# All HGRN2 heads through the levels together: scores by half chunks, mask copies over all partitions

## Chip, cores and metric

The kernel runs on one core of a Trainium2 chip. The metric is the device time of one execution in microseconds; the reported time is the median of three runs. In the trace the engines are PE (TensorE's matmuls), PEld (its weight loads), DVE (VectorE), ACT (ScalarE), POOL (GpSimd) and SP (SyncE, which issues most of the DMAs).

## What is computed

The reference is a trunk of two layers on 512 tokens of width 1024, all in float32. Each layer adds the output projection of three token mixers (RG-LRU, retention and HGRN2) to x, and then a gated feed-forward block with a short convolution.

```python
for l in range(DEPTH):
    proj = rmsnorm(x, norm1_w[l]) @ w_in[l]
    lx, lg, rq, rk, rv, rg, hq, hf, hi, hg = jnp.split(proj, split_idx, axis=-1)
    y_lru = rglru_group(lx, lg, ...)
    y_ret = retention_group(rq, rk, rv, rg, ret_norm_w[l])
    y_hg = hgrn2_group(hq, hf, hi, hg, lb_all[l], hg_norm_w[l])
    x = x + jnp.concatenate([y_lru, y_ret, y_hg], axis=-1) @ w_out[l]
    x = x + conv_ffn(rmsnorm(x, norm2_w[l]), ...)
return rmsnorm(x, final_norm_w)
```

HGRN2 has four heads of width 64. With a forget gate f, keys k, queries q and values v its recurrence is S_t = diag(f_t) S_{t-1} + k_t v_t^T, and the output is o_t = S_t^T q_t. Retention has the same form with a fixed decay for each head. Both outputs are normalised for each head and gated.

## The kernel before

**Precision and projections.** A large product is made of three fp32r matmuls (`mm3`, lines 319 to 321): high times high, high times low and low times high. `split_w` splits every weight tile into a high part (ACT, `wh`) and a low part (DVE, `wl`). An input projection takes 24 matmuls of 512 columns per tile of 128 outputs; there are 24 tiles in a layer, in the order of `WIN` (line 63). Four PSUM banks (`NMM`) hold projections until `evac` multiplies them by the norm of the tokens and writes them to one of four `ev` tiles. All other matmuls are plain float32 and go through `small` (line 325). Each such product stands in the trace as two instructions.

**Order.** `Flow` is a planner: Python generators (chains) yield between operations, and every operation has an assumed cost (`Timed`). The main chain issues the large matmuls; whenever a chain's operands are due by the planner's clock, its small matmuls are put into TensorE's order between two of the large ones. Each engine executes its list in that order. If an operand is later on the chip than was planned, TensorE waits with everything behind it.

**HGRN2.** `hg_chain(ft)` runs once for each of two pairs of heads; a pair fills the 128 partitions (64 per head). Scores inside a chunk of 128 tokens are built in seven levels (`LEVELS` 1, 2, ... 64). At each level 8 products (4 at level 64) of the keys with every second block of queries go to the PSUM tile `hg_pl`. GpSimd then multiplies half of the keys by products of forget gates (`kl`), VectorE multiplies half of the queries (`qr`) and the gates by each other (`p2`), and VectorE writes the scores under a mask into `st` by `copy_predicated`, once for each half of the partitions. The next level's products need the new keys and queries. Behind the levels come `key_rows` (transposes, `k_tps`), `states` (`k_mps`, `k_sv`), `mix_values` (`k_o`) and a norm over each head (`head_norm`).

**The rest of a mixer stage.** Retention (`ret_chain`, for each pair of heads) needs rotated queries and keys (`rope`), forms scores per head (`rt_ps`), and shares `states` and `mix_values`; its norm (`head_norm_cols`) computes a reciprocal root on a few columns (`hc_rc`, `rsqrt_cols`) and spreads it by products with the identity (`hn_rps`). The LRU (`lru_conv`, `lru_batch`, `scan`) starts its convolutions when both HGRN2 pairs are done; at its end GpSimd multiplies four tiles (`qp<-qp,lr_g` in the trace, line 850) ahead of four VectorE scans.

**Ends.** The last layer's last down projection (`down_and_norm`) runs in two halves of the tokens; `finish` computes the reciprocal root of the final norm on two columns (`fn_v`, `fn_rc`), spreads it (`fn_rps`), scales x and stores it. At the start `FIRST` (line 31) is the order of the first loads: tiles of x and halves of the first two weight tiles.

## Time and profile before

| | us |
|---|---|
| median of three runs | 1194.06 |
| lowest and highest run | 1193.67, 1194.18 |
| profiled execution, its own time | 1192.48 |
| its span, first to last instruction | 1190.7 |
| PE busy in the span | 1171.8 |
| DVE busy | 810.9 |
| ACT busy | 511.3 |
| POOL busy | 101.9 |

Busy times are unions of an engine's instructions. Matmuls are pipelined: one that follows another starts before its predecessor has ended, and the distance from start to start is what it costs. The two layers have the same stages: mixers with the input projection (from 6.32 and 594.80 us), the output projection (from 191.75 and 773.48 us), and the feed-forward block.

### The profile page before, as it was taken

To read this page: it belongs to the slowest core of one execution; us is meant where nothing else is said; L and a number is where in the kernel's file an instruction comes from. 1 tells how busy PE (TensorE), PEld (TensorE's weight loads), DVE (VectorE), ACT (ScalarE), POOL (GpSimd) and SP (SyncE) were. 2 spreads that over 40 slices of the span, in tenths; PEclk is the share of its full clock that TensorE was granted. 3 is DMA by queue.
4 is the path that set the end of the run, shared out by engine and by line. 5 is a ranking of instruction groups with operands and counts; after the bars stand their busy time and mean duration, and the time that the engine had idled before them with its cause. 6 is when DMAs were issued, how large, how long until landed. Compare 5 with 4: busy or idle time off the path is not lost.

```text
span 1190.7 us, 15377 instructions
## 1 busy us (share of the span) xinstructions
PE 1171.8 (98%) x6062; PEld 968.4 (81%) x6062; DVE 810.9 (68%) x1220; ACT 511.3 (43%) x689; POOL 101.9 (9%) x85
## 2 busy tenths in 40 slices
PE   9999989999999999999999999999999999999996
PEld 8787778888888888888897877788888888888886
DVE  7998678667775576465679775964877646655746
ACT  6425574454443343242441446644544423433423
POOL 0221230000000000000323111400000000000001
PEclk9999999999999999999999999999999999999998
DMA  7222213233323322322332121323232233233221
GB/s 257 92 81 64 80 42 118 89 97 98 103 79 96 112 92 81 117 83 80 115 124 63 63 89 54 98 97 107 89 104 91 80 115 96 81 107 102 80 83 73
DMA packets 36312, 112.29 MB, mean 94 GB/s; under 512 B 4496, under 2 KB 4752, under 8 KB 36240
## 3 DMA queue, kind: packets, MB, share of 16 engines
q1 hardware_dynamic: 34416, 108.95, 29.2%
q10 hardware_dynamic: 1824, 2.37, 0.7%
q8 instruction: 47, 0.77, 0.3%
q14 instruction: 25, 0.20, 0.1%
HBM read 107.10 MB, written 2.10 MB: 92 GB/s over the span
## 4 chain that ended last, share of the span: by engine, by line
PE 92%; DVE 5%; issue 1%; DMA 0%; POOL 0%; ACT 0%; POOLq 0%; ACTq 0%
PE pps L319 19%; PE pps L321 18%; PE pps L320 18%; PE dps L319 7%; PE dps L321 7%; PE dps L320 7%; PE ops L321 2%; PE ops L320 2%; PE ops L319 2%; DVE qp L185 2%; PE k_o L325 1%; PE vps L319 1%; PE lr_ps L325 1%; DVE st L185 1%; PE vps L320 1%; PE vps L321 1%
## 5 line engine op out<-in xcount | busy, mean ns | idle before, releaser
L319 PE MATMUL pps<-xh,wh 128*128 128x512 f32 x1024 | 406.3, 397 | 1.3 <-ACT wh L185 1.3
L321 PE MATMUL pps<-xh,wl 128*128 128x512 f32 x1024 | 399.3, 390 | 0.6 <-DVE wl L185 0.6
L320 PE MATMUL pps<-xl,wh 128*128 128x512 f32 x1024 | 399.1, 390 | 0.0
L185 ACT ACTIVATE wh<-raw 128x1024 fp32r<-128x1024 f32 (+3 forms) x211 | 204.7, 973 | 145.8 <-PE dps L320 103.3
L185 DVE TENSOR_TENSOR wl<-raw,wh 128x1024 fp32r<-128x1024 f32 (+3 forms) x211 | 242.6, 1153 | 20.4 <-ACT wh L185 19.8
L319 PEld LDWEIGHTS pps<-xh,wh 128*128 128x128 f32 x1024 | 192.5, 188 | 44.4 <-issue 2.9
L321 PEld LDWEIGHTS pps<-xh,wl 128*128 128x128 f32 x1024 | 192.4, 188 | 42.0 <-DVE wl L185 1.2
L320 PEld LDWEIGHTS pps<-xl,wh 128*128 128x128 f32 x1024 | 192.5, 188 | 39.7 <-issue 1.2
L185 DVE SCALAR_TENSOR_TENSOR hs<-pps,rb 128x512 f32<-128x512 f32 x88 | 60.5, 691 | 128.7 <-PE pps L321 128.7
L319 PE MATMUL dps<-gh,wh 128*128 128x512 f32 x320 | 124.5, 389 | 0.0
L320 PE MATMUL dps<-gl,wh 128*128 128x512 f32 x320 | 124.5, 389 | 0.0
L321 PE MATMUL dps<-gh,wl 128*128 128x512 f32 x320 | 124.5, 389 | 0.0
L185 DVE TENSOR_TENSOR x<-x,dps 128x512 f32<-128x512 f32 (+1 forms) x72 | 45.1, 627 | 107.3 <-PE dps L321 106.6
L185 ACT ACTIVATE cg<-hs,prm 128x512 f32<-128x512 f32 x44 | 35.9, 817 | 81.1 <-DVE hs L185 76.4
L320 PEld LDWEIGHTS dps<-gl,wh 128*128 128x128 f32 x320 | 60.1, 188 | 12.5
L321 PEld LDWEIGHTS dps<-gh,wl 128*128 128x128 f32 x320 | 60.1, 188 | 12.5
L319 PEld LDWEIGHTS dps<-gh,wh 128*128 128x128 f32 x320 | 60.1, 188 | 12.4
L185 DVE SCALAR_TENSOR_TENSOR cvv<-hs,prm,cvv 128x511 f32<-128x511 f32 x88 | 65.9, 748 | 1.8
L185 DVE SCALAR_TENSOR_TENSOR cg<-hs,prm,cg 128x511 f32<-128x511 f32 x88 | 65.8, 748 | 1.5
L185 ACT ACTIVATE cg<-cg 128x512 f32<-128x512 f32 x44 | 27.8, 632 | 86.9 <-DVE cg L185 86.9
L185 ACT ACTIVATE gh<-cvv 128x512 fp32r<-128x512 f32 x44 | 27.8, 631 | 76.6 <-DVE cvv L185 76.6
L185 ACT ACTIVATE cvv<-hs,prm 128x512 f32<-128x512 f32 x44 | 35.9, 817 | 33.0 <-DVE hs L185 33.0
(210 smaller groups left out, 1353.3 us busy)
## 6 DMA issues: line engine op xcount, KB each, us to landing
raw<-in_wup_dram SPq DMA_DIRECT2D x88, 512.0 KB, 3.5
raw<-in_win_dram SPq DMA_DIRECT2D x46, 512.0 KB, 3.5
raw<-in_wdn_dram SPq DMA_DIRECT2D x48, 384.0 KB, 3.0
raw<-in_wout_dram SPq DMA_DIRECT2D x16, 512.0 KB, 3.5
raw<-in_wdn_dram SPq DMA_DIRECT2D x16, 256.0 KB, 2.6
x<-in_x_dram SPq DMA_DIRECT2D x8, 256.0 KB, 5.0
sw<-ev ACTq DMA_DIRECT2D x32, 64.0 KB, 2.5
out_dram<-hs SPq DMA_DIRECT2D x7, 256.0 KB, 2.0
```

The source lines that it names most:

```text
L185: return fn(*args, **kw)
L319: T.matmul(out=ps, lhsT=ah, rhs=bh, start=start, stop=False)
L320: T.matmul(out=ps, lhsT=ah, rhs=bl, start=False, stop=False)
L321: T.matmul(out=ps, lhsT=al, rhs=bh, start=False, stop=stop)
L325: T.matmul(**kw)
```

## The change

HGRN2 is rebuilt for all four heads at once. The projections of both pairs' gates and queries (`hf`, `hq`) stand ahead of the HGRN2 values in `WIN`. `hg_query(ft)` prepares the queries of a pair; one `hg_chain` runs the levels over tiles `qa`, `fa`, `ka`, `sta` that hold both pairs side by side. A level has 16 products in one PSUM bank (8 at level 64, which alternate between the two halves of the partitions). Scores stand in `sta` by half chunks: both halves of a chunk use the same 64 columns on their own 64 partitions, so that one `copy_predicated` covers all 128 partitions; level 32 is copied by ACT without a mask. The product with the values is therefore also made by half chunks, against values `vz` with zeros in the other half. The key products `kl` and the product of queries and keys move from POOL to DVE, as do the four products ahead of the LRU's scans.

Retention's scores are issued with the two heads of a pair in turn, into two PSUM banks. Its states are products of full width whose cross terms are multiplied by zero, so the product with the state is also one of full width. `head_norm_cols` writes the last step of the reciprocal root spread over 64 columns (`hx`) and uses products of full width.

`finish` takes a square root on ACT and a reciprocal and one correction step on DVE; the table of the square root is loaded at the first tile of the last down projection. The output tiles have buffers of their own, the scaling on ACT is done as x becomes known, and the last store is split in two, on two queues. The first weight half is loaded from SP's queue. A smaller scratch area of the DMAs frees memory for the pool `low`, which holds `hx`, `r_sv` and `vz`. The planner's price of `copy_predicated` is raised.

```diff
 WIN = (
-    [("f", 2304), ("f", 2048), ("v", 2560, 0), ("v", 2560, 1), ("f", 2432), ("f", 2176)]
+    [("f", 2304), ("f", 2048), ("f", 2432), ("f", 2176), ("v", 2560, 0), ("v", 2560, 1)]
     + [("f", 1024), ("f", 1280), ("v", 1536, 0), ("v", 1536, 1), ("f", 1152), ("f", 1408)]
...
 WNAMES = (
-    [("hf", 0), ("hq", 0), "hv", None, ("hf", 1), ("hq", 1)]
+    [("hf", 0), ("hq", 0), ("hf", 1), ("hq", 1), "hv", None]
     + [("rq", 0), ("rk", 0), "rv", None, ("rq", 1), ("rk", 1)]
...
-    hc = rsqrt_cols(mp, ps, [128, NC, 2], "hc", bufs=2)
+    hx = low.tile([128, NC, 2, 64], F32, name="hc_x")
+    rsqrt_cols(mp, ps, [128, NC, 2], "hc", bufs=2, out=hx)
...
     for c in range(NC):
-        for h in range(2):
-            small(0.12, out=ps[64 * h:64 * h + 64, c * 128:(c + 1) * 128],
-                  lhsT=hc[:, c, h:h + 1].to_broadcast([128, 64]), rhs=ident, skip_group_check=True)
+        small(0.22, out=ps[:, c * 128:(c + 1) * 128],
+              lhsT=hx[:, c].rearrange("p h n -> p (h n)"), rhs=ident)
...
+    for c in range(1, NC):
+        cs = slice(c * 128, (c + 1) * 128)
+        small(0.22, out=ops[:, cs], lhsT=sv[:, c - 1, :], rhs=q[:, cs],
+              start=c == 1, stop=False, skip_group_check=True)
...
-            hs = slice(64 * h, 64 * h + 64)
-            small(0.11, out=ops[hs, cs], lhsT=sv[hs, c - 1, :], rhs=q(c, h),
...
+qa = mp.tile([128, 2, 2 * S], F32, name="qp")
+fa = mp.tile([128, 2 * S], F32, name="f")
+ka = mp.tile([128, 2 * S], F32, name="k")
+
+
+sta = mp.tile([128, 4 * NC, 128], F32, name="st")
...
-    qk = mp.tile([128, S], F32, name="sq", bufs=2)
-    G.tensor_tensor(out=qk, in0=q, in1=kt, op=ALU.mult)
+    yield None
+    qk = sg
+    V.tensor_tensor(out=qk, in0=q, in1=ka[:, ts], op=ALU.mult)
+    V.tensor_tensor(out=q, in0=q, in1=fa[:, ts], op=ALU.mult)
+    yield None
     for h in range(2):
         hs = slice(64 * h, 64 * h + 64)
-        V.tensor_tensor(out=qp[hs, h, :], in0=q[hs, :], in1=f[hs, :], op=ALU.mult)
+        A.activation(out=qa[hs, h, ts], in_=q[hs, :], func=AF.Copy)
...
+def hg_chain():
+    for ft in range(2):
+        yield has(("hq", ft))
+    p = fa
...
+            pl = yield from psum([128, NB, 2, 32], "hg_pl")
+        for c in range(NB):
+            for b in range(1 if s == 64 else 2):
+                m = 64 * (c % 2) if s == 64 else 64 * b
+                q0 = c * 128 + 64 * b
+                n = 128 if s == 64 else 64
+                rhs = qa[:, :, q0:q0 + n].rearrange("p h (b t s) -> p h b t s", t=2, s=s)[:, :, :, 1, :]
+                small(0.1 if s == 64 else 0.05,
+                      out=pl[m:m + 64, c // 2 if s == 64 else c].rearrange("p h (b s) -> p h b s", s=s),
+                      lhsT=ka[:, q0:q0 + 64], rhs=rhs, skip_group_check=True)
...
+        nb2 = S // s
         pv = p[:, 0:2 * nb2].rearrange("p (b t) -> p b t", t=2)
-        kl = kt.rearrange("p (b t s) -> p b t s", t=2, s=s)[:, :, 0, :]
-        G.tensor_tensor(out=kl, in0=kl, in1=pv[:, :, 1:2].to_broadcast([128, nb2, s]), op=ALU.mult)
-        go = fl.mark
-        fl.mark, fl.last = fl.now, None
-        qr = qp.rearrange("p h (b t s) -> p h b t s", t=2, s=s)[:, :, :, 1, :]
+        kl = ka.rearrange("p (b t s) -> p b t s", t=2, s=s)[:, :, 0, :]
+        V.tensor_tensor(out=kl, in0=kl, in1=pv[:, :, 1:2].to_broadcast([128, nb2, s]), op=ALU.mult)
+        qr = qa.rearrange("p h (b t s) -> p h b t s", t=2, s=s)[:, :, :, 1, :]
         V.tensor_tensor(out=qr, in0=qr,
                         in1=pv[:, :, 0].unsqueeze(1).unsqueeze(3).to_broadcast([128, 2, nb2, s]), op=ALU.mult)
-        go = max(go, fl.mark)
-        p2 = mp.tile([128, S // 2], F32, name=f"hg_p{ft}", bufs=2)
+        go = fl.mark
+        p2 = mp.tile([128, S], F32, name="hg_p", bufs=2)
         V.tensor_tensor(out=p2[:, 0:nb2], in0=pv[:, :, 0], in1=pv[:, :, 1], op=ALU.mult)
         if s == 64:
-            A.activation(out=st[0:64, :, 64:128], in_=pl[0:64].rearrange("p c h t -> p (c h) t"), func=AF.Copy)
+            for m in range(2):
+                A.activation(out=sta[0:64].rearrange("p (c m h) q -> p c m h q", m=2, h=2)[:, :, m, :, 64:128],
+                             in_=pl[64 * m:64 * m + 64], func=AF.Copy)
+        elif s == 32:
+            for m in (0, 64):
+                A.activation(out=sta[m:m + 32, :, 32:64], in_=pl[m:m + 32].rearrange("p c h q -> p (c h) q"),
+                             func=AF.Copy)
         else:
-            for m in (0, 64):
-                V.copy_predicated(
-                    out=st[m:m + 64, :, m:m + 64].rearrange("p g (b t s) -> p g b t s", t=2, s=s)[:, :, :, 1, :],
-                    mask=msk[m:m + 64, i, :].rearrange("p (b s) -> p b s", s=s).unsqueeze(1).to_broadcast(
-                        [64, NC * 2, 32 // s, s]),
-                    data=pl[m:m + 64].rearrange("p c h (b s) -> p (c h) b s", s=s),
-                )
+            V.copy_predicated(
+                out=sta[:, :, 0:64].rearrange("p g (b t s) -> p g b t s", t=2, s=s)[:, :, :, 1, :],
+                mask=msk[:, i, :].rearrange("p (b s) -> p b s", s=s).unsqueeze(1).to_broadcast(
+                    [128, 2 * NB, 32 // s, s]),
+                data=pl.rearrange("p c h (b s) -> p (c h) b s", s=s),
+            )
         drop(sm)
         p = p2
         if s == 1:
-            evt.add(("f_free", ft))
+            evt.add("f_free")
         yield go - fl.now
...
+    pss = []
+    for ft in range(2):
+        pss.append((yield from psum([128, S], "k_o")))
+    for ft in range(2):
+        ops = pss[ft]
+
+        for b in range(2):
+            for c in range(NC):
+                for h in range(2):
+                    d0 = (2 * ft + h) * 64
+                    small(0.1, out=ops[64 * h:64 * h + 64, c * 128 + 64 * b:(c + 1) * 128],
+                          lhsT=vz[:, c, b, d0:d0 + 64], rhs=sta[:, ft * NB + 2 * c + h, 0:128 - 64 * b],
+                          start=b == c == 0, stop=False, skip_group_check=True)
+        for c in range(1, NC):
+            for h in range(2):
+                small(0.11, out=ops[64 * h:64 * h + 64, c * 128:(c + 1) * 128], lhsT=sv[:, ft, c - 1, :],
+                      rhs=qa[:, h, ft * S + c * 128:ft * S + (c + 1) * 128],
+                      start=False, stop=False, skip_group_check=True)
...
     def scan(j):
-        G.tensor_tensor(out=xcs[j], in0=xcs[j], in1=gts[j][1], op=ALU.mult)
+        V.tensor_tensor(out=xcs[j], in0=xcs[j], in1=gts[j][1], op=ALU.mult)
...
-    st = mp.tile([128, 2, NC, 128], F32, name="st", bufs=2)
+    if not rst:
+        rst.append(mp.tile([128, 2, 2, NC, 128], F32, name="st"))
+    st = rst[0][:, ft]
+    pss = []
+    for h in range(2):
+        pss.append((yield from psum([128, NC, 128], "rt_ps")))
+
+    for c in range(NC):
+        cs = slice(c * 128, (c + 1) * 128)
+        for h in range(2):
+            hs = slice(64 * h, 64 * h + 64)
+            small(0.15, out=pss[h][:, c, :], lhsT=rk[hs, cs], rhs=rq[hs, cs])
+    yield None
...
-        hs = slice(64 * h, 64 * h + 64)
-        ps = yield from psum([128, NC, 128], "rt_ps")
...
-            cs = slice(c * 128, (c + 1) * 128)
-            small(0.11, out=ps[:, c, :], lhsT=rk[hs, cs], rhs=rq[hs, cs])
...
     def finish(sps, ts, hf):
-        rc = rsqrt_cols(fp, sps, [128, 2], "fn")
+
+        rc, t, v = (fp.tile([128, 2], F32, name=f"fn_{i}", bufs=1) for i in "rtv")
+        A.activation(out=t, in_=sps, func=AF.Sqrt, bias=eps)
+        V.reciprocal(out=rc, in_=t)
+        V.tensor_scalar(out=v, in0=sps, scalar1=EPS, scalar2=None, op0=ALU.add)
+        V.tensor_tensor(out=t, in0=rc, in1=rc, op=ALU.mult)
+        V.scalar_tensor_tensor(out=t, in0=t, scalar=-0.5, in1=v, op0=ALU.mult, op1=ALU.mult)
+        V.scalar_tensor_tensor(out=rc, in0=t, scalar=1.5, in1=rc, op0=ALU.add, op1=ALU.mult)
...
-        A.activation(out=rb, in_=rps, func=AF.Copy)
+        V.tensor_copy(out=rb, in_=rps)
...
+            if m < KD - 2 or not hf:
+                nc.sync.dma_start(out=out[:, hf, m:m + 2, :], in_=yo)
+            else:
+                for i in range(2):
+                    (nc.sync, nc.scalar)[i].dma_start(out=out[:, hf, m + i, :], in_=yo[:, i, :])
...
+            if hf == m == 0:
+
+                A.activation(out=fp.tile([128, 1], F32, name="fn_tab", bufs=1), in_=eps, func=AF.Sqrt)
...
-        (nc.sync if e else nc.scalar).dma_start(out=raws[e // 2][:, c], in_=wlist[e // 2][:, c])
+        nc.sync.dma_start(out=raws[e // 2][:, c], in_=wlist[e // 2][:, c])
...
+    nc = bacc.Bacc("TRN2", target_bir_lowering=False, num_devices=1, dynamic_dma_scratch_size=1024)
```

## Rows read from the trace of the kernel before

**Rows 1.** The page, part 1: busy us (share of the span) xinstructions.
```profile
PE 1171.8 (98%) x6062; PEld 968.4 (81%) x6062; DVE 810.9 (68%) x1220; ACT 511.3 (43%) x689; POOL 101.9 (9%) x85
```

**Rows 2.** Stretches: their length, then busy (instructions) of PE, PEld, DVE, ACT, POOL.
```profile
core 0: us, PE busy (x) PEld busy (x) DVE busy (x) ACT busy (x) POOL busy (x), PEclk, DMA share, GB/s
60.00:92.00 32.00, 30.61 (x307) 26.20 (x306) 30.90 (x68) 8.93 (x15) 9.83 (x11) 1.00 0.23 72
150.00:180.00 30.00, 26.32 (x144) 21.21 (x143) 22.00 (x30) 22.08 (x29) 10.37 (x7) 0.94 0.18 54
222.00:600.00 378.00, 378.00 (x1669) 313.06 (x1668) 238.90 (x309) 152.42 (x197) 13.04 (x9) 1.00 0.32 98
```

**Rows 3.** PE in order of time, one level: start us, length us, line, tiles, count.
```profile
40.46 0.40 PE L321 MATMUL pps<-xh,wl 128*128 128x512 f32 x1
40.79 0.69 PE L325 MATMUL hg_pl<-qp,k 128*64 128x64 f32 x16
...
41.74 0.39 PE L320 MATMUL pps<-xl,wh 128*128 128x512 f32 x1
```

**Rows 4.** PE in order of time: other small groups, each with the second large matmul behind.
```profile
90.67 1.09 PE L325 MATMUL hg_pl<-qp,k 128*64 128x128 f32 x8
...
92.03 0.40 PE L320 MATMUL pps<-xl,wh 128*128 128x512 f32 x1
...
97.38 1.16 PE L325 MATMUL rt_ps<-f 64*128 64x128 f32 x8
...
98.80 0.39 PE L320 MATMUL pps<-xl,wh 128*128 128x512 f32 x1
...
124.90 1.09 PE L325 MATMUL hn_rps<-csm,hc_rc 128*64 128x128 f32 x16
...
126.26 0.40 PE L320 MATMUL pps<-xl,wh 128*128 128x512 f32 x1
```

**Rows 5.** PE grouped: busy us, mean ns | idle us before them, and what ended it.
```profile
L321 PE MATMUL pps<-xh,wl 128*128 128x512 f32 x1024 | 399.3, 390 | 0.6 <-DVE wl L185 0.6
...
L325 PE MATMUL hg_pl<-qp,k 128*64 128x64 f32 x384 | 16.4, 227 | 2.2 <-DVE hg_p L185 1.2 <-DVE qp L185 1.0
...
L325 PE MATMUL hn_rps<-csm,hc_rc 128*64 128x128 f32 x64 | 5.3, 316 | 3.7 <-DVE hc_rc L185 3.7
...
L325 PE MATMUL hg_pl<-qp,k 128*64 128x128 f32 x32 | 4.3, 277 | 1.0 <-DVE hg_p L185 1.0
```

**Rows 6.** DVE and POOL in order of time, ahead of hn_rps at 175.47.
```profile
169.25 1.07 DVE L185 TENSOR_SCALAR hc_rc<-hc_v 128x8 int32<-128x8 int32 x1
...
174.05 0.17 DVE L185 SCALAR_TENSOR_TENSOR hc_rc<-hc_nt,hc_rc 128x8 f32<-128x8 f32 x1
...
168.50 5.49 POOL L185 TENSOR_TENSOR qp<-qp,lr_g 128x512 f32<-128x512 f32 x4 [0.45 <-ACT qp L185]
```

**Rows 7.** DVE grouped by shape: busy us, mean ns | idle us before them.
```profile
L185 DVE TENSOR_TENSOR wl<-raw,wh 128x1024 fp32r<-128x1024 f32 x150 | 188.3, 1259 | 20.3 <-ACT wh L185 19.8 <-DMA sw<-ev 0.4
...
L185 DVE COPY_PREDICATED st<-msk,hg_pl 64x256 f32<-64x256 uint8 x48 | 25.6, 533 | 0.9
...
L185 DVE TENSOR_TENSOR qp<-qp,hg_p 128x512 f32<-128x512 f32 x24 | 18.0, 752 | 0.5 <-PE hg_pl L325 0.5
```

**Rows 8.** DVE in order of time: the last norm, first and last of 12 steps.
```profile
1180.67 0.16 DVE L185 TENSOR_SCALAR fn_v<-fn_ps 128x2 f32<-128x2 f32 x1 [0.81 <-PE fn_ps L325]
...
1182.84 0.16 DVE L185 SCALAR_TENSOR_TENSOR fn_rc<-fn_nt,fn_rc 128x2 f32<-128x2 f32 x1
```

**Rows 9.** ACT in order of time: a square behind exponentials, a table load, a sigmoid.
```profile
160.36 0.62 ACT L185 ACTIVATE sq<-rt_on 128x512 f32<-128x512 f32 x1
...
161.95 1.28 ACT L185 ACT_TABLE_LOAD   x1
163.24 0.63 ACT L185 ACTIVATE sq<-ev 128x512 f32<-128x512 f32 x1
```

**Rows 10.** ACT in order of time at the start: issue and use of the first weight half.
```profile
1.18 0.45 ACTq L1226 DMA_DIRECT2D raw<-in_win_dram  x1
...
5.85 0.72 ACT L185 ACTIVATE wh<-raw 128x256 fp32r<-128x256 f32 x2 [0.41 <-DMA raw<-in_win_dram]
```

More of the change, by code (lines that the diff above doesn't have):

```diff
@@ L333, in drop, with rsqrt_cols @@
         fl.later(fl.mark - fl.now, slots.give)
[L336 removed]
+    def rsqrt_cols(pool, ps, shape, name, bufs=1, out=None):
         v = pool.tile(shape, F32, name=f"{name}_v", bufs=bufs)
@@ L345, in rsqrt_cols @@
                         op0=ALU.mult, op1=ALU.add)
-        for _ in range(3):
+        for i in range(3):
             V.tensor_tensor(out=t, in0=r, in1=r, op=ALU.mult)
             V.scalar_tensor_tensor(out=t, in0=t, scalar=-0.5, in1=v, op0=ALU.mult, op1=ALU.mult)
-            V.scalar_tensor_tensor(out=r, in0=t, scalar=1.5, in1=r, op0=ALU.add, op1=ALU.mult)
+            if i == 2 and out is not None:
+                t, r = (a.unsqueeze(len(shape)).to_broadcast(shape + [out.shape[-1]]) for a in (t, r))
+            V.scalar_tensor_tensor(out=out if i == 2 and out is not None else r, in0=t, scalar=1.5, in1=r,
+                                   op0=ALU.add, op1=ALU.mult)
         return r
@@ L662, in mix_values @@
                     d0 = (2 * ft + h) * 64
[L663 to L669 removed]
+                    small(0.13, out=ops[64 * h:64 * h + 64, cs], lhsT=v[:, c, d0:d0 + 64], rhs=sc(c, h),
                           start=False, stop=False, skip_group_check=True)
@@ L718, in hg_chain @@
             yield None
-            st = mp.tile([128, NC * 2, 128], F32, name="st", bufs=2)
-            def diag():
-                dps = yield from psum([128, NC, 2], "hg_dps")
-                for c in range(NC):
-                    small(0.21, out=dps[:, c, :], lhsT=qk[:, c * 128:(c + 1) * 128], rhs=hind)
-                drop(sqs)
-                yield None
-                V.tensor_tensor(out=st,
-                                in0=dps.rearrange("p c h -> p (c h)").unsqueeze(2).to_broadcast([128, NC * 2, 128]),
-                                in1=ident.unsqueeze(1).to_broadcast([128, NC * 2, 128]), op=ALU.mult)
-                drop(sm)
-                evt.add(("diag", ft))
@@ L782, in hg_chain @@
-            o = mp.tile([128, S], F32, name="hg_on", bufs=2)
-            A.activation(out=o, in_=ops, func=AF.Copy)
+            v, vz = vv["h"], vv["z"]
+            ps = yield from psum([128, 2, NC - 1, 64], "k_mps")
+            for ft in range(2):
+                for c in range(NC - 1):
+                    for h in range(2):
+                        hs = slice(64 * h, 64 * h + 64)
+                        d0 = (2 * ft + h) * 64
+                        small(0.06, out=ps[hs, ft, c, :], lhsT=krs[ft][:, c, hs], rhs=v[:, c, d0:d0 + 64],
+                              skip_group_check=True)
@@ new lines, in hg_chain @@
+            yield None
+            sv = mp.tile([128, 2, NC - 1, 64], F32, name="k_sv")
+            V.tensor_copy(out=sv[:, :, 0, :], in_=ps[:, :, 0, :])
+            for ft in range(2):
+                for c in range(1, NC - 1):
+                    V.scalar_tensor_tensor(out=sv[:, ft, c, :], in0=sv[:, ft, c - 1, :],
+                                           scalar=p[:, ft * NC + c:ft * NC + c + 1], in1=ps[:, ft, c, :],
+                                           op0=ALU.mult, op1=ALU.add)
@@ L790, in mixers @@
+            yield None
+            for ft in range(2):
+                o = mp.tile([128, S], F32, name="hg_on", bufs=2)
+                A.activation(out=o, in_=pss[ft], func=AF.Copy)
+                drop(sm)
+                evt.add(("hg_done", ft))
+                fl.spawn(head_norm(o, hon, ("h", ft)))
+            yield None
         lw = mp.tile([128, 2, 4, 128], F32, name="lw")
         nc.sync.dma_start(out=lw, in_=lruw[l])
-        xc2, xcs, hst = {}, {}, {}
+        xc4, xcs, hst = [], {}, {}
@@ L879, in rope @@
                 nc.scalar.dma_start(out=sw[b * 32:(b + 1) * 32, :], in_=a[src:src + 32, :])
-            r = mp.tile([128, S], F32, name="k" if ft else "f", bufs=2)
+            if ft not in rots:
+                rots[ft] = mp.tile([128, 2, S], F32, name="fk"[ft])
+            r = rots[ft][:, kind == "rk", :]
             V.tensor_tensor(out=r, in0=a, in1=cc("cos"), op=ALU.mult)
```

148 lines of the change are left out of this document (69 added, 79 removed).

## The prediction

> **What bounds the kernel now.** I read the page first. TensorE is busy for 98% of the span [rows 1], so the time is the sum of what TensorE is given plus the little that it waits. Next came the table of stretches [rows 2]: in the feed-forward stretch, 222 to 600 us, TensorE never idles and 1669 matmuls take 378.00 us, 0.227 us for one of 512 columns. The change does not touch that stretch. In the mixer stretch from 60 to 92 us TensorE idles 1.4 us of 32 while VectorE works 30.90, and from 150 to 180 us TensorE idles 3.7 us and its granted clock averages 0.94. So two things can be won: short matmuls in the mixers, which TensorE pays for in full, and waits in the mixers.
>
> The TensorE timeline then prices the short matmuls. Around one level of one head pair [rows 3], large matmuls that start at 40.46 and 41.74 enclose the 16 instructions (8 products) of hg_pl. The distance is 1.28 us, two large steps are 0.45, so the level costs 0.83. From its own start to the second large matmul it is 0.95, so 0.12 comes off that distance; the other groups [rows 4] are read with the same 0.12. A level of 64 (4 products of 128 columns): 1.36 - 0.12 = 1.24. hn_rps (8 products of 128 columns into alternating halves of the partitions): 1.24. rt_ps (4 products with 64 rows each): 1.42 - 0.12 = 1.30.
> From these come three prices. hn_rps and a level are both 8 alternating products and differ by 0.41 us, which is 64 more columns each, so a 64-column product costs 0.051, a 128-column one 0.103. What is left, 0.83 - 0.41 = 0.42, is the entry into a group of half-array products. Products that do not alternate cost (1.30 - 0.42)/4 = 0.22 for 128 columns.
>
> Last, the waits. By the grouped TensorE list [rows 5] the level groups wait 2.2 + 1.0 us, hn_rps 3.7 and a projection 0.6 for its weight: 7.5 us. The half clock after the hn_rps wait adds up to 0.06 x 30 = 1.8 us [rows 2]. Why hn_rps waits is seen on VectorE [rows 6]: an operation on 8 elements takes 1.07 us at 169.25 and 0.17 at 174.05; the long ones run while GpSimd does its four multiplies qp<-qp,lr_g from 168.50 to 173.99.
>
> **The change part by part, TensorE.** Per layer, in us. Levels 1 to 32: today 12 groups of 0.83 = 9.96; afterwards 6 groups of 16 products, 0.42 + 16 x 0.051 = 1.24 each = 7.4; gain 2.5. Level 64: two groups of 1.24 become one of 8 alternating products, 0.42 + 8 x 0.103 = 1.24; gain 1.2. HGRN2 states: two groups become one, gain one entry, 0.4. HGRN2 values: today 2 x (14 x 0.103 + 0.42) = 3.7; afterwards 28 of 128 and 16 of 64 columns in one group, 4.1; loss 0.4. Retention scores: today 4 x 1.30 = 5.2; afterwards two groups whose products alternate between the upper and lower 64 rows. No row shows that alternation at full width. Bounds: like alternating halves of columns, 1.24 a group (gain 2.7), or no overlap, 0.42 + 8 x 0.22 = 2.2 (gain 0.8). I take 2.7, because hn_rps, the nearest row with two alternating halves, overlaps. Retention norm: 2 x 1.24 becomes 2 x 4 full-width products of 0.22; gain 0.7. Retention states and values: within 0.1. The sum is 7.1 a layer, 14.2 for two. In the timeline eight of today's groups stand against another and already share an entry; I expect about half as many to do so afterwards, which takes 4 x 0.4 = 1.6 off. **TensorE: -12.6.**
> A rule on the disputed term: the Trainium skill, TensorE: Matmul & The Clock Gate, Part 3 (Packing small matmuls), says that products in different row groups overlap, and reports 3.07 times for four of them. No trace here shows it for 64 x 128. By the page the gain is near 2.7 a layer, by the far bound 0.8.
>
> **VectorE and GpSimd.** These lie beside TensorE and count only through waits. By the groups [rows 7] a layer's 24 mask copies (12.8 us) become 5 of twice the length (at most 5.3), the 14 query products (10.5) become 7 of twice the length (7 x 1.26 = 8.8, by the 1024-wide row), and the key products leave GpSimd for VectorE (7 x 0.75 = 5.3). The scan products go the same way (4 x 0.75 = 3.0). VectorE's load stays about even; what it loses is GpSimd beside it. ScalarE gains copies, but it works only 8.93 of 32 us there [rows 2].
> Waits. The 3.7 of hn_rps and its 1.8 of clock should go, because the GpSimd multiply that stretches VectorE's small operations is gone: -5.5. Next late there is VectorE's queue itself, 3.0 us longer by the four products, which stand ahead of weight splits. The 3.2 at the levels come from one serial chain, and a chain for all heads asks half as often; bounds 0 and 6.4, I keep half: -1.6. Half of the 0.6 goes: -0.3. One wait is added: with hf, hq of both pairs projected ahead of the values, all four accumulators are taken until the norm is known, and the value tile behind them on TensorE's queue waits; price about one evacuation [rows 7], 0.75, +0.7. **Waits: -6.7**, with -2 and -9 as bounds.
>
> **Ends.** The last rsqrt is 12 dependent VectorE steps, 1180.67 to 1183.00 = 2.33 us [rows 8]; afterwards a ScalarE square root and 5 such steps. Five steps are 1.0; the square root has no row, between 0.2 and 0.5 with its hand-over; I take 0.4: -0.9. The last store as two halves on two queues: between +0.2 and -0.5, taken -0.3. **Tail -1.2**, between -0.6 and -1.6. The same chain in the first half is under matmuls and worth nothing; its price without that cover would be the same 0.9. The square root's table is loaded early, beside matmuls, for 1.28 [rows 9].
> A rule against this part: the Trainium skill, ScalarE: Activation LUTs, What ACT_TABLE_LOAD costs, puts every switch of set at 2.66 us with its drain. The trace disagrees: load at 161.95, next operation at 163.24 [rows 9], so 1.29 in all.
> Start: ScalarE waits 0.41 us for the first weight half [rows 10], issued at 1.18 behind the parameters. On SyncE's queue it goes out at about the same time but ahead of x1; the loads behind it, on the same queue, each go out one issue (0.45) later. Between -0.4 and +0.4, taken **-0.3**. The smaller DMA scratch and the pool below it only move addresses: nothing, as no row shows an operation that they touch.
>
> **Sum.** 1192.5 (the profiled execution) - 12.6 - 6.7 - 1.2 - 0.3 = 1171.7. The runs' median, 1194.1, lies 1.6 above that execution: 1173.3. With all bounds at the good end (-14.2, -9, -1.6, -0.4) it is 1168.9, at the bad end (-8.8, -2, -0.6, +0.4) 1183.1.
>
> **Rivals.**
> A, waits are moved, not removed: VectorE is still near full in the levels [rows 2], and the four scan products take the place of GpSimd's. Then waits give 1 us instead of 6.7: 1179. For it: VectorE's load is even. Against: the hn_rps wait has GpSimd beside it, not load.
> B, the retention scores do not overlap: 3.8 us more, 1177.
> C, slower: the chain for all heads is exposed. From a level's matmuls to the next, VectorE alone now does a key product (0.75) and a query product (1.26), 2.0 us, 14 times: if TensorE has nothing ordered between two levels it waits 28 us, 1201. It decides from 1.5 us of wait per level, since the rest of the gain is about 21. Against: today's 28 level groups wait 3.2 in all [rows 5], 0.1 each, because projection matmuls lie between.
> D, waits clear to the bound and the full 14.2 is won: 1169.
> E, the early square-root table does not hold Square, so ScalarE loads tables back and forth and one load of 1.28 lands in the tail in place of the 0.9 gained: 1175.5. Against: [rows 9] is preceded by Square under the exponential's table without a load.
>
> **How the numbers follow.** Forecast 0.50 (1173), A 0.22, B 0.07, C 0.08, D 0.08, E 0.05. A measurement of this kernel tells about 0.2%, 2.4 us, from no change. Of C, 0.02 ends within that and 0.06 above; all else is faster: 0.92. The range takes in A, B, D, E and the bounds: 1166 to 1183.
>
> **What would show it.** Level groups of 32 instructions that cost about 1.24; rt_ps x16 in place of two x8 in about 1.24; hn_rps x8 with no idle before; no 1 us VectorE operations on 8 elements; fn steps of 1.4. Wrong if TensorE's idle time in the mixers is above 8 us, if hg_pl waits more than 1 us per level, or if the large matmuls' 0.227 changes.

## The result and the profile after

The changed kernel takes 1175.87 us (median of four runs, 1175.76 to 1176.60); the kernel before, beside it, 1193.87 (1192.06 to 1194.18). The ratio is 0.9854, with a 95% interval from 0.9837 to 0.9871: 1.5% faster, forecast 1173. Its profiled execution took 1176.6 us with a span of 1174.8, which is 15.9 less than before.

Part 1 of the page of the changed kernel, which answers [rows 1]:

```profile
PE 1160.0 (99%) x6046; PEld 965.5 (82%) x6046; DVE 780.3 (66%) x1162; ACT 522.9 (45%) x706; POOL 59.9 (5%) x51
```

Four stretches of it, with the columns of [rows 2]; the third is the start of layer 0's output projection, the last is feed-forward:

```profile
60.00:92.00 32.00, 32.00 (x295) 27.70 (x295) 24.91 (x58) 8.20 (x14) 1.45 (x1) 1.00 0.30 91
150.00:180.00 30.00, 28.93 (x135) 23.59 (x133) 24.30 (x39) 22.24 (x32) 3.22 (x2) 1.00 0.23 71
178.00:194.00 16.00, 13.35 (x53) 10.57 (x52) 12.66 (x18) 6.28 (x9) 0.00 (x0) 0.89 0.37 129
210.00:586.00 376.00, 376.00 (x1661) 311.40 (x1660) 236.38 (x308) 151.11 (x195) 8.85 (x6) 1.00 0.30 96
```

In the levels (60 to 92 us) TensorE no longer idles. It idles from 178 to 194 us instead, and the granted clock falls there. TensorE's list by groups, for [rows 5], says for what: nothing waits in hg_pl any more, almost nothing in hn_rps, and 2.6 us before a matmul of the output projection, where nothing waited before.

```profile
L323 PE MATMUL pps<-xh,wl 128*128 128x512 f32 x1024 | 399.2, 390 | 0.7 <-DVE wl L185 0.7
L322 PE MATMUL ops<-xl,wh 128*128 128x512 f32 x128 | 50.7, 396 | 2.6 <-DVE xl L185 2.6
L327 PE MATMUL hg_pl<-qp,k 128*64 128x64 f32 x384 | 13.8, 225 | 0.0
L327 PE MATMUL hn_rps<-csm,hc_x 128*128 128x128 f32 x32 | 4.3, 277 | 0.1
L327 PE MATMUL hg_pl<-qp,k 128*64 128x128 f32 x32 | 2.2, 279 | 0.0
```

TensorE in order of time, as [rows 3, 4]: a level of all heads, the retention scores of a pair, a retention norm, and that wait.

```profile
45.88 0.39 PE L323 MATMUL pps<-xh,wl 128*128 128x512 f32 x1
46.20 1.16 PE L327 MATMUL hg_pl<-qp,k 128*64 128x64 f32 x32
...
47.63 0.40 PE L322 MATMUL pps<-xl,wh 128*128 128x512 f32 x1
...
97.77 0.40 PE L323 MATMUL pps<-xh,wl 128*128 128x512 f32 x1
98.09 1.16 PE L327 MATMUL rt_ps<-f 64*128 64x128 f32 x16
...
99.52 0.39 PE L322 MATMUL pps<-xl,wh 128*128 128x512 f32 x1
...
123.93 0.40 PE L323 MATMUL pps<-xh,wl 128*128 128x512 f32 x1
124.16 1.06 PE L327 MATMUL hn_rps<-csm,hc_x 128*128 128x128 f32 x8
...
125.29 0.39 PE L322 MATMUL pps<-xl,wh 128*128 128x512 f32 x1
...
178.62 0.39 PE L321 MATMUL ops<-xh,wh 128*128 128x512 f32 x1
181.66 0.79 PE L322 MATMUL ops<-xl,wh 128*128 128x512 f32 x1 [2.65 <-DVE xl L185]
182.25 0.63 PE L323 MATMUL ops<-xh,wl 128*128 128x512 f32 x1
182.67 0.63 PE L321 MATMUL ops<-xh,wh 128*128 128x512 f32 x1
...
185.58 0.40 PE L323 MATMUL ops<-xh,wl 128*128 128x512 f32 x1
```

Read as in the prediction: of the large matmuls around a level, the last ahead of it starts at 45.88 and the second behind it at 47.63; 1.75 less two steps of 0.227 is 1.30 for 16 products, where two groups of 8 cost 1.66. The scores cost 99.52 - 97.77 - 0.45 = 1.30, the norm 0.91. The wait costs more than its 2.65: from 178.62 to 185.58 twelve steps take 6.96 instead of 2.72, because steps at half the granted clock (0.43) follow it: 4.2 in all.

What the operand is late for is seen on VectorE, in order of time at the end of layer 0's mixers:

```profile
173.49 0.69 DVE L185 TENSOR_TENSOR lr_g<-lr_g,ev 128x512 f32<-128x512 f32 x1 [0.46 <-DVE lr_g L185]
174.10 1.22 DVE L185 TENSOR_TENSOR_SCAN lr_g<-lr_a,qp 128x512 f32<-128x512 f32 x1
175.23 1.20 DVE L185 TENSOR_TENSOR wl<-raw,wh 128x1024 fp32r<-128x1024 f32 x1
176.35 2.33 DVE L185 TENSOR_TENSOR_SCAN lr_g<-lr_a,qp 128x512 f32<-128x512 f32 x2
178.60 0.67 DVE L185 TENSOR_TENSOR lr_g<-lr_g,ev 128x512 f32<-128x512 f32 x1
179.18 0.69 DVE L185 TENSOR_TENSOR ev<-pps,rb 128x512 f32<-128x512 f32 x1
179.78 1.22 DVE L185 TENSOR_TENSOR wl<-raw,wh 128x1024 fp32r<-128x1024 f32 x1
180.91 1.29 DVE L185 TENSOR_TENSOR xl<-hg_on,xh 128x512 fp32r<-128x512 f32 x2
```

The high part of that operand was there by 175.4 (ScalarE makes it), but the low part, xl<-hg_on, stands behind scans, an evacuation and a weight split.

### The profile page after: what moved, and what is told of

Read it like the earlier page. It is cut to its first block, busy times and chain, and to the rows that moved or that the text cites. A ratio compares the mean times of both kernels' runs of the same rounds, so it can differ in the third digit from the quotient of the medians.

```text
span 1174.8 us, 15202 instructions
## 1 busy us (share of the span) xinstructions
PE 1160.0 (99%) x6046; PEld 965.5 (82%) x6046; DVE 780.3 (66%) x1162; ACT 522.9 (45%) x706; POOL 59.9 (5%) x51
## 4 chain that ended last, share of the span: by engine, by line
PE 95%; DVE 3%; issue 1%; DMA 0%; SPq 0%; ACT 0%; POOL 0%; POOLq 0%; DVEq 0%
PE pps L321 19%; PE pps L323 19%; PE pps L322 19%; PE dps L321 7%; PE dps L323 7%; PE dps L322 7%; PE ops L322 3%; PE ops L323 3%; PE ops L321 2%; PE vps L321 1%; PE vps L322 1%; PE k_o L327 1%; PE vps L323 1%; PE hg_pl L327 1%; PE lr_ps L327 1%; DVE qp L185 1%
## 5 line engine op out<-in xcount | busy, mean ns | idle before, releaser
L321 PEld LDWEIGHTS pps<-xh,wh 128*128 128x128 f32 x1024 | 192.3, 188 | 43.2 <-issue 2.4
L323 PEld LDWEIGHTS dps<-gh,wl 128*128 128x128 f32 x320 | 60.1, 188 | 12.6
L322 PE MATMUL ops<-xl,wh 128*128 128x512 f32 x128 | 50.7, 396 | 2.6 <-DVE xl L185 2.6
```

The source lines that it names most:

```text
L321: T.matmul(out=ps, lhsT=ah, rhs=bh, start=start, stop=False)
L322: T.matmul(out=ps, lhsT=ah, rhs=bl, start=False, stop=False)
L323: T.matmul(out=ps, lhsT=al, rhs=bh, start=False, stop=stop)
```

## The experiments

All runs stand beside the kernel before; times are medians, to be held against the changed kernel's 1175.87. Executions of one kernel differ by up to 3.4 us (run 11, 1177.42 to 1180.84), and the kernel before has medians of 1192.4 to 1192.8 beside the runs, 1193.87 beside the changed kernel. Differences of about 2 us are therefore read together with the traces.

**1. The four products ahead of the scans back on GpSimd.**

```diff
     def scan(j):
-        V.tensor_tensor(out=xcs[j], in0=xcs[j], in1=gts[j][1], op=ALU.mult)
+        G.tensor_tensor(out=xcs[j], in0=xcs[j], in1=gts[j][1], op=ALU.mult)
```

> The changed kernel with one edit: the four products ahead of the LRU's scans go back from VectorE to GpSimd; all else stays. In the changed kernel the output projection of layer 0 waits 2.65 us at 181.66 us for the low part of its first operand, whose split stands on VectorE behind these products, scans and weight splits (4.4 us in all with the half clock that follows). Theory L (VectorE has too much to do at the end of the mixers): its queue is 2.5 us shorter, the split comes at about 178.4 instead of 180.91, the wait is gone, and the time falls by 3 to 4.4 us, to 1171.5 to 1173. Theory G (GpSimd beside VectorE is what stretches its short operations, as the prediction had it for the norm's wait): the steps of the retention norm grow to about 1 us again wherever the products stand beside them and hn_rps waits 2 to 4 us; net 1174 to 1177. Which one it is shows in the idle time before hn_rps (0 to 0.5, or over 2 us) and before the output projection (below 0.5 us under both).

1178.26 us, ratio 0.9881 (0.9864 to 0.9897). The projection's wait is gone, but hn_rps waits 4.29 us, again with half clock behind it. VectorE and GpSimd of this run in order of time:

```profile
158.99 1.07 DVE L185 TENSOR_SCALAR hc_rc<-hc_v 128x8 int32<-128x8 int32 x1
...
161.35 0.17 DVE L185 TENSOR_TENSOR hc_nt<-hc_rc 128x8 f32<-128x8 f32 x1
161.55 1.30 DVE L185 SCALAR_TENSOR_TENSOR hc_nt<-hc_nt,hc_v 128x8 f32<-128x8 f32 x1
...
166.57 0.17 DVE L185 SCALAR_TENSOR_TENSOR hc_rc<-hc_nt,hc_rc 128x8 f32<-128x8 f32 x1
```

```profile
158.06 3.22 POOL L185 TENSOR_TENSOR ev<-ev,sq 128x512 f32<-128x512 f32 x2 [10.63 <-ACT sq L185]
161.53 4.99 POOL L185 TENSOR_TENSOR qp<-qp,lr_g 128x512 f32<-128x512 f32 x4 [0.25 <-POOL ev L185]
```

Six of the steps on 8 elements take 1.07 to 1.30 us while GpSimd multiplies and 0.17 in its one pause and after it: theory G. The Trainium skill, SBUF — State Buffer, Who interferes with whom, has a rule for this: VectorE with two SBUF inputs, or in a two-port mode, and GpSimd exclude each other for a whole instruction. The trace agrees, each stretched step lasting about one GpSimd product. So the move to VectorE is worth 2.4 us net, 2.0 by the profiled executions: it removes a wait that costs 6.7 and brings one of 4.2.

**2. Other order on VectorE, same work.**

```diff
     def scan(j):
+        if j >= 2:
+            yield lambda: all(k in y for k in (4, 5, 6, 7))
```

> The changed kernel with one edit: the third and the fourth LRU scan (with their products) are put into the order only after the splits of the HGRN2 and retention outputs. VectorE has exactly the same work, in another order. Theory O (only the order of VectorE's list is wrong): the output projection of layer 0 starts without a wait, 3 to 4.4 us are won, 1171.5 to 1173. Theory L (too much work): in the changed kernel VectorE works without a break from 163.81 to 190.13 us, where the last split ends; the last operand would be needed at 178.7 + 13 x 0.68 = 187.6 us, so the wait comes back about 2 us long before the last two operands of the projection's first pair of tiles, and the time is 1174 to 1176.

1175.81 us, ratio 0.9861 (0.9846 to 0.9875), as theory L has it. The projection now starts at once and waits 2.15 us at 188.91 for a later operand. Order alone does not help; VectorE's work from 164 us on does not fit ahead of the projection.

**3. Both.** The edits of 1 and 2 together.

> Both edits of the two runs before: products ahead of the scans on GpSimd, and the last two scans behind the splits. Theory L: work and order are both eased, no wait of over 0.3 us is left in the output projection of layer 0; 1171.5 to 1172.5, no slower than either edit alone. Theory G: as for the first run, hn_rps waits 2 us or more and the time is above 1174. If the last two scans now come too late (GpSimd's products take about 1.4 us each), a wait of 0.5 to 2 us stands before the last two operands and the time is 1173 to 1174.5.

1178.20 us, ratio 0.9881 (0.9866 to 0.9895), with hn_rps waiting 4.24: theory G once more, and the second edit adds nothing.

**4. Levels in two groups.**

```diff
     for c in range(NB):
+        if c == NC:
+            yield 1.5
         for b in range(1 if s == 64 else 2):
```

> The changed kernel with one edit: the 16 products of a level go out as two groups of 8 with projection matmuls between them (4 and 4 at level 64), so the number of products and all work of the other engines stay as they are. Theory E (a group pays an entry of 0.42 us whatever it holds, which is the larger part of the prediction's gain at the levels): 14 more groups cost 14 x 0.42 = 5.9 us, less where a half comes to stand beside another group, so 4 to 6 us more than the changed kernel: 1179.5 to 1182; a half level costs 0.42 + 8 x 0.051 = 0.83. Theory P (the price lies in the products and not in the groups): under 1.5 us more, 1176 to 1177.5, and a half level costs 0.65. If the later start of a level's VectorE work delays the next level, idle time before hg_pl shows it; it was 0.0 in the changed kernel and is counted apart.

1203.25 us, ratio 1.0090 (1.0075 to 1.0105), outside both ranges. TensorE in order of time, a half level and the output projection:

```profile
45.42 0.39 PE L323 MATMUL pps<-xh,wl 128*128 128x512 f32 x1
45.74 0.69 PE L327 MATMUL hg_pl<-qp,k 128*64 128x64 f32 x16
...
46.70 0.39 PE L322 MATMUL pps<-xl,wh 128*128 128x512 f32 x1
...
188.77 0.50 PE L322 MATMUL ops<-xl,wh 128*128 128x512 f32 x1 [2.13 <-DVE xl L185]
...
200.36 0.79 PE L322 MATMUL ops<-xl,wh 128*128 128x512 f32 x1 [9.26 <-DVE xl L185]
```

The price is theory E's: a half level costs 46.70 - 45.42 - 0.45 = 0.83, two of them 1.66 against 1.30, so a group's entry is 0.36 to 0.42 and all 14 levels lose 5.1. The other 22 us are what neither theory had: hg_pl still waits nothing, but each level is later, values (k_o) come 13 us later, and the projections wait for VectorE 11.4 us in layer 0 and 5.5 in layer 1 (with 2.7 more at an hn_rps), with half clock behind the longer waits (mean granted clock 0.988, 0.996 in the changed kernel).

**5. Retention scores one head after the other.**

```diff
-    for c in range(NC):
-        cs = slice(c * 128, (c + 1) * 128)
-        for h in range(2):
+    for h in range(2):
+        for c in range(NC):
+            cs = slice(c * 128, (c + 1) * 128)
```

> The changed kernel with one edit: the score products of retention go out one head after the other instead of in turn; they keep their two PSUM banks and stay one group. Theory R (products on the upper and the lower 64 rows overlap when they alternate, and that is what the gain of 2.7 us a layer rests on): a group of eight costs 0.42 + 8 x 0.22 = 2.2 us instead of the 1.30 measured in the changed kernel, and four groups make the kernel 3.6 us slower: 1179 to 1180. Theory M (the gain came from merging two groups into one, and the order within does not matter): a group stays at 1.3 to 1.5 us and the time within 0.8 us of the changed kernel's 1175.9.

1178.61 us, ratio 0.9879 (0.9862 to 0.9895). TensorE in order of time:

```profile
96.77 0.40 PE L323 MATMUL pps<-xh,wl 128*128 128x512 f32 x1
97.10 1.71 PE L327 MATMUL rt_ps<-f 64*128 64x128 f32 x16
...
99.07 0.40 PE L322 MATMUL pps<-xl,wh 128*128 128x512 f32 x1
```

A group costs 1.85, 0.55 more than in turn; four groups give 2.2 of the 2.7 us between the medians. Theory R holds in kind: the two halves of the rows overlap. In size it was too large: a product that does not alternate costs (1.85 - 0.42)/8 = 0.18, not 0.22.

This run's profiled execution took 1176.76 us, only 0.2 more than that of the changed kernel; its other three took 1178.6 to 1178.8. The trace shows why. The projection waits as long as in the changed kernel, but no half clock follows, which cost 1.6 in the changed kernel's profile (4.2 less the wait):

```profile
178.77 0.39 PE L321 MATMUL ops<-xh,wh 128*128 128x512 f32 x1
181.78 0.50 PE L322 MATMUL ops<-xl,wh 128*128 128x512 f32 x1 [2.62 <-DVE xl L185]
182.11 0.40 PE L323 MATMUL ops<-xh,wl 128*128 128x512 f32 x1
```

**6. The planner's old price of copy_predicated.**

```diff
-c = 0.07 + n * (1.65e-3 if op == "copy_predicated" else 0.52e-3 if op in ...
+c = 0.07 + n * (0.52e-3 if op in ...
```

> The changed kernel with one edit: the planner's price of copy_predicated is as before, 0.60 us instead of 0.91 for a copy that takes 0.69 in the trace. No instruction changes, only places in the order. Theory N (the waits before the levels went because one chain asks half as often, as predicted): hg_pl still waits less than 0.5 us in all, and with the levels planned up to 0.3 us earlier each the time is 1174 to 1176. Theory P (the waits went because the planner was told the truth about the copies): hg_pl waits 1 to 3 us in all, with the half clock behind some of them, 1177 to 1180.

1170.57 us (1170.07 to 1170.59), ratio 0.9810 (0.9795 to 0.9824): 5.3 faster than the changed kernel, faster than either theory allowed. The new price removed no wait. With the old one TensorE does not wait in either mixer stage after 22 us. One place that differs is seen on ScalarE in order of time, first in the changed kernel, then in this run:

```profile
146.75 0.72 ACT L185 ACTIVATE lr_a<-lr_g,lamc 128x512 f32<-128x512 f32 x1
...
154.08 0.72 ACT L185 ACTIVATE lr_g<-lr_g,lamc 128x512 f32<-128x512 f32 x1
154.71 0.62 ACT L185 ACTIVATE sq<-rt_on 128x512 f32<-128x512 f32 x1
```

```profile
141.10 0.63 ACT L185 ACTIVATE sq<-rt_on 128x512 f32<-128x512 f32 x1 [0.87 <-DVE rt_on L185]
...
143.99 0.72 ACT L185 ACTIVATE lr_a<-lr_g,lamc 128x512 f32<-128x512 f32 x1
```

With the raised price the square of the second retention output stands behind the LRU's twelve exponentials, and its norm falls into VectorE's full stretch, beside GpSimd.

**7. Key products back on GpSimd.**

```diff
-    V.tensor_tensor(out=kl, in0=kl, in1=pv[...].to_broadcast([128, nb2, s]), op=ALU.mult)
+    G.tensor_tensor(out=kl, in0=kl, in1=pv[...].to_broadcast([128, nb2, s]), op=ALU.mult)
+    go = fl.mark
+    fl.mark, fl.last = fl.now, None
...
-    go = fl.mark
+    go = max(go, fl.mark)
```

> The changed kernel with one edit: the key products of the seven levels go back from VectorE to GpSimd, beside the query products. The run with split levels showed that a delay of the HGRN2 chain comes out at the end of the mixers nearly in full (chain 13 us later, output projection of layer 0 11.4 us late). Theory C (a level's length is its work on VectorE): 7 x 0.6 us leave VectorE and the chain ends up to 4 us earlier, the wait of 2.65 us before the output projection is gone, 1171.5 to 1174. Theory G (what GpSimd does beside VectorE is paid for twice): GpSimd needs about 1.4 us for 512 columns, so a level gets no shorter, VectorE's short operations and mask copies stretch to 1.0 to 1.3 us beside it, hg_pl waits again 1 to 4 us in all, and the time is 1176 to 1181.

1175.54 us, ratio 0.9853 (0.9838 to 0.9868): no difference, and a mixture. Level 64 of layer 0 starts at 74.47 instead of 81.15, so the levels do get shorter (C), although beside GpSimd's products a query product takes 2.02 us instead of 1.22 (G). The 1.31 of a mask copy there is not GpSimd's doing: the copies of the first two levels take that long in the changed kernel too, with GpSimd idle, and those of the other three 0.7. Levels wait 1.9 in all and the projection still 1.22. The 6.7 us of the chain are not passed on: the LRU's exponentials end at 155.7, even later than in the changed kernel (154.8). Copies of the second and the third level in the changed kernel, VectorE in order of time:

```profile
55.00 1.32 DVE L185 COPY_PREDICATED st<-msk,hg_pl 128x512 f32<-128x512 uint8 x1
...
60.83 0.70 DVE L185 COPY_PREDICATED st<-msk,hg_pl 128x512 f32<-128x512 uint8 x1
```

**8. Both ends undone.**

```diff
-    nc.sync.dma_start(out=raws[e // 2][:, c], in_=wlist[e // 2][:, c])
+    (nc.sync if e else nc.scalar).dma_start(out=raws[e // 2][:, c], in_=wlist[e // 2][:, c])
...
-    A.activation(out=t, in_=sps, func=AF.Sqrt, bias=eps)
...
+    rc = rsqrt_cols(fp, sps, [128, 2], "fn")
```

> The changed kernel with its two ends undone: the first weight half is loaded from ScalarE's queue again, and the last norm uses the twelve steps on VectorE instead of the square root. They are read apart by their places. Tail: from the last fn_ps product to the first fn_rps product 2.4 us instead of 1.14, so +1.3 by theory S (the square root shortens the end by what its chain is shorter). Start: theory Q (the loads behind the first one pay what it gains): the first large product starts about 1.1 us later but its third x tile lands about 1.2 us earlier, the 48th large product ends 0.3 to 0.6 us earlier than in the changed kernel. Theory F (the first product sets the start): the 48th ends 0.5 to 1.1 us later. Time: by S and Q 1176.3 to 1177.3, by S and F 1177.5 to 1178.5.

1179.69 us (1178.62 to 1180.64), ratio 0.9887 (0.9872 to 0.9902). The tail, TensorE in order of time, first changed, then undone:

```profile
1164.77 0.58 PE L327 MATMUL fn_ps<-csm,ssq 128*128 128x1 f32 x4 [0.94 <-DVE ssq L185]
...
1167.38 0.71 PE L327 MATMUL fn_rps<-csm,fn_r 128*128 128x128 f32 x4 [1.14 <-DVE fn_r L185]
```

```profile
1164.70 0.58 PE L327 MATMUL fn_ps<-csm,ssq 128*128 128x1 f32 x4 [1.47 <-DVE ssq L185]
...
1168.59 1.22 PE L327 MATMUL fn_rps<-csm,fn_rc 128*128 128x128 f32 x4 [2.42 <-DVE fn_rc L185]
```

Theory S: 1.14 against 2.42, 1.3 us for the square root. The start is not settled: the 48th large product ends at 17.51 us here, at 18.18 in the changed kernel, and between 17.21 and 17.94 in ten other profiles with the new start, so the start's effect is below its scatter. By the profiled executions the undone ends cost 2.0 us, 1.8 of them in these two waits. The medians lie 3.8 apart because the four executions form two pairs (1178.62 and 1178.83, 1180.55 and 1180.64) and the median falls between them. The higher pair has the lower mean granted clock (0.994 against 0.995 and 0.996), but only one of the lower pair was traced, so what made it longer stays open.

**9. Prices as changed, but the square ahead of the exponentials.**

```diff
     A.activation(out=sq, in_=src, func=AF.Square)
+    evt.add(("sq", key))
...
     yield has(("on", ("h", 1)))
+    yield has(("sq", ("r", 1)))
```

> The changed kernel, the planner's prices as it has them, with one edit: the twelve exponentials of the LRU are put into ScalarE's order only after the square of the second retention output. In the changed kernel that square stands behind them (154.71 us in layer 0, its operand was there at 147.1), so the norm's 13 steps fall at 159 to 164 us, into the stretch where VectorE is full and GpSimd multiplies; in the run with the old price the square stands ahead of them and all mixer waits are gone. Theory S (this one place in the order is what the price did): the norm's steps fall near 150 us, each takes 0.17 us, the wait before the output projection of layer 0 is below 0.5 us and the time is 1171 to 1173. Theory K (it is the levels themselves, planned up to 0.3 us earlier each, 2.4 us at the last): the square alone changes little, 1175 to 1176.5, and the wait before the output projection stays over 1.5 us.

1172.96 us, ratio 0.9832 (0.9818 to 0.9847). The norm's steps run from 148.8 to 151.7 us at 0.17 each. That one place is worth 2.9 of the 5.3 us: theory S in time, but the projection still waits 1.22, so it is not all that the price did. Of the 2.9, about 1.6 is the half clock, which does not follow the shorter wait.

**10. Old price, and the last norm's output pairs apart.**

```diff
     (nc.sync, nc.scalar)[i].dma_start(out=out[:, hf, m + i, :], in_=yo[:, i, :])
+    if hf == 0:
+        yield None
```

> The changed kernel with two edits: the planner's old price of copy_predicated, and in the last norm the planner may again order other work between the output pairs of the first half of the tokens (as the kernel before does). In all runs with the square root the final sum of squares waits 0.94 us for VectorE, which has five output products of the first half in a row just before; before the change that wait was 0.18. Theory T (those five stand in the way): the wait before fn_ps falls to 0.2 to 0.4 us, the tail shortens by 0.6 to 0.8, and the time is 1169.8 to 1170, the fastest of all. Theory V (the last tile's own chain of add, square and add sets it): fn_ps still waits over 0.8 us and the time is that of the run with the old price alone, 1170.6.

1168.92 us (1168.63 to 1169.40), ratio 0.9799 (0.9784 to 0.9813): the fastest of all. The 0.94 before fn_ps is gone; 0.10 is left before its second group, where the kernel before waits 0.06 and 0.12. So theory T. Against run 6 the end comes 0.8 us sooner after the last large product; the rest of the 1.65 is not explained by these traces.

**11. The planner's price of copy_predicated at 0.68 us.** The factor 1.65e-3 becomes 1.2e-3.

> The changed kernel with one edit: copy_predicated is priced at 0.68 us, near the 0.69 of the trace, between the old 0.60 and the changed kernel's 0.91. In layer 0 ScalarE's order then has the square of the second retention output ahead of the exponentials, as with the old price. Theory S (the place of that square decides): 1169.5 to 1172.5, no wait over 0.5 us before the output projection of layer 0. Theory A (any price above the old one delays the levels and costs in proportion, 5.3 us for 0.31): about a quarter of it, 1171.5 to 1172.5 with a wait of 0.7 us or more; the two differ in that wait, and a time above 1173 speaks against both.

1177.64 us, ratio 0.9880 (0.9862 to 0.9898). Both theories fall. The square stands ahead of the exponentials and the norm is done by 154.5, and yet the projection waits 3.02 and 1.43 us. Here the exponentials themselves come late: they end at 159.5. Nor was this price nearer the truth. The 0.69 of the expectations is a copy of the last three levels; the first two take 1.30 to 1.32 (run 7), the ten copies of the changed kernel 0.95 on average, so that 0.91 is nearest to the mean and no single price fits all of them.

**12. The kernel before, with the edit of run 9.**

> The kernel before, with the square of the second retention output put ahead of the LRU's exponentials on ScalarE and nothing else. Its hn_rps wait is 3.7 us in all and costs up to 1.8 more in clock; the prediction blames GpSimd's four products beside the norm's small steps. Theory S (the place of the square brings the norm to the same time as those products): the norm comes some 10 us earlier, ahead of the products, the wait is gone although GpSimd still does all its work, and the kernel before gains 3 to 5.5 us: 1187.5 to 1190. Theory G alone (GpSimd's work has to go, wherever the norm stands): it still waits over 2 us and the time is 1191.5 to 1194.

1190.38 us against 1192.41 in the same job, ratio 0.9985 (0.9975 to 0.9994). Theory S for the wait: hn_rps waits nothing, all steps take 0.17, although GpSimd keeps its products. Only 2.0 us are won: the output projection now waits 1.77 and a projection 0.63 for its weight's split. The profiled execution, 1192.79, is the longest of ten (from 1190.02); its 48th large product ends at 20.17 us against 17.64 in the kernel before, so 2.5 us of it are a late start. Before the change, too, a cured norm uncovers VectorE at the end of the mixers.

## Why the prediction was right, and where it was off

The kernel is faster, as forecast; the time is inside the range, 2.9 us above the forecast. That it came so near is in part chance: the same instructions in two orders take 1170.6 (run 6) and 1175.9 us, one on either side of 1173. By the profiled executions the sum was -20.8, measured -15.9.

**TensorE, -12.6 forecast, -12.3 measured.** The groups of small products, priced one by one as above with their waits taken out, go from 42.9 to 37.0 us in layer 0 and from 43.2 to 36.8 in layer 1. A level costs 1.30 (forecast 1.24), level 64 1.23 (1.24), scores 1.30 (1.24), a norm 0.91 (0.88), values 4.37 (4.1). Runs 4 and 5 show the two mechanisms behind it, the entry into a group and overlapping row halves; rival B is out. The Trainium skill's rule on row groups (TensorE: Matmul & The Clock Gate, Part 3) is borne out in kind: eight products in turn cost 1.30, one half after the other 1.85.

**Waits, -6.7 forecast, -3.4 measured: the term that was mis-sized.** The hn_rps waits went (-4.9 of a forecast -5.5) and all of the level waits (-3.2, forecast -1.6). The weight's wait of 0.65 stayed, the bank's (+0.7, read off the row of a query product) did not come, a gap of 0.30 at the LRU's products in layer 1 costs 0.5. What ate the gain is the new wait at the output projection, +4.2, of which 1.6 is half clock that did not follow the same wait in run 5. The prediction named the place, "next late there is VectorE's queue itself", and gave it no price; rival A named the cause and priced it in full, at 6. The truth lies between.

Two steps failed. First, the planner's price was an edit without an instruction and got no term. Run 6 shows 5.3 us for it, run 9 that 2.9 of them come with one square's place. Second, the cover was taken as given. TensorE's part of layer 0's mixers shrank by 13.1 us (output projection from 191.75 to 178.62), while the last exponential of the LRU, behind which VectorE still has its products, scans, gates and splits, moved only from 160.5 to 154.8. The waits follow that distance:

| layer 0 of | last exponential ends | projection begins | between | it then waits |
|---|---|---|---|---|
| before | 160.5 | 191.8 | 31.3 | 0 |
| run 1 | 154.6 | 185.1 | 30.6 | 0 |
| run 6 | 152.0 | 177.7 | 25.7 | 0 |
| run 10 | 151.7 | 177.3 | 25.6 | 0 |
| run 2 | 154.4 | 178.2 | 23.8 | 2.15 |
| after | 154.8 | 178.6 | 23.8 | 2.65 |
| run 7 | 155.7 | 179.2 | 23.6 | 1.22 |
| run 12 | 166.3 | 189.7 | 23.5 | 1.77 |
| run 9 | 156.5 | 177.6 | 21.1 | 1.22 |
| run 11 | 159.5 | 177.6 | 18.1 | 4.45 |
| run 4 | 168.7 | 186.3 | 17.6 | 11.39 |

From 25.6 us up nothing waits; below, something always does, and between 21 and 24 us least where the norm's steps lie ahead of that stretch (runs 7, 9, 12). Run 11 fits as well: its norm is early, its exponentials are late. Runs 3, 5 and 8 agree: distances of 30.7, 23.9 and 23.8 go with waits of 0, 2.62 and 2.64. So does layer 1: there the distance is 26.9 us or more in every trace but run 4's and the projection starts without a wait (run 2, with its scans moved back, waits 0.30 later on); in run 4 it is 16.9 and the wait 5.5. No run changes the distance alone, so it is the best reading of fourteen traces, not a proof. It is also what rival C was about, only not at the levels, which wait nothing in the changed kernel, but at the end of the chain that they feed.

Rival A's ground, a load of VectorE that stays "about even", was a misreading: the load fell from 810.9 to 780.3 us. By the groups, as in [rows 7], mask copies lost 16.1 us and query products 3.4, key products brought 8.5 and scan products 5.0; the other 24.6 are not followed here. VectorE has less to do in all and is waited for even so, because what counts is the work between the last exponential and the projection.

**Tail, -1.2 forecast, -0.9 measured.** The square root is worth 1.3 instead of 0.9, but the final sum waits 0.94 where it waited 0.06 and 0.12 before (together the 0.18 of run 10's expectation); run 10 shows why and takes it back. **Start, -0.3 forecast**: 0.5 later in the changed kernel's profile, no effect beyond the scatter over all runs. With -12.3, -3.4, -0.9 and +0.5 the sum is -16.1; 0.2 is unassigned.

Of what was to show the steps, one failed: two steps on 8 elements still take 1.07 and 1.22 us, beside GpSimd's gate products (ev<-ev,sq) that the change left there. Rivals D (near the time of runs 6 and 10, but not of this kernel) and E (no table load in the tail) are out.

## What to carry to other kernels

Price short half-array products by group: here about 0.4 us for entering one, then 0.05 us a product of 64 columns and 0.10 to 0.11 one of 128, as long as neighbours use different halves of columns or rows. When a bound engine's work shrinks, measure again what its length was covering: here the distance from the last exponential to the next stage fell below 25 us and a fifth of the expected gain went into a new wait. And treat a planner's price list as code: an edit that issued no instruction cost 5.3 of the 22 us that the rebuild won without it. The price nearest to the copies' mean (0.91) and one between (0.68) both did worse than the lowest (0.60), so a price has to be tried and the waits read again.

## What the runs showed of the hardware that was not expected

- Beside GpSimd, VectorE's single-input steps on 8 elements stretch too (TENSOR_SCALAR 1.07 us in run 1, 0.17 in run 9), while hc_v, which reads only PSUM, took 0.16 at the same time.
- A wait is not always followed by half clock: behind 2.65 (changed kernel), 2.64 (run 8), 4.29 (run 1) and 9.26 us (run 4) the large steps took 0.43 for a while; behind 2.62 (run 5), 2.15 (run 2) and 2.13 us (run 4) they stayed at 0.23. Between runs 5 and 8 the waits differ by 0.02 us; what decides, no run shows.
- A copy_predicated of 128x512 takes 1.30 to 1.32 us at the first two levels and 0.69 to 0.72 at the other three, in the same kernel and with GpSimd idle. No run isolates why.
- Products on 64 rows that do not alternate cost 0.18 each in a group of eight (run 5), less than the 0.22 read from groups of four [rows 4].
